# An encoder layer's recurrence: block-diagonal state in the chain, and small matmuls on different tiles of the array issued alternately

## The chip, the cores and the metric

The kernel runs on one core of a Trainium2 chip. Its time is device microseconds (us) of one launch. TensorE is named PE in the profile, VectorE DVE, ScalarE ACT, GpSimd POOL, and SyncE's DMA queue SP.

## What is computed

One layer of a hybrid encoder over 512 frames and 16 meta tokens, 1024 wide: a token mixer (sparse attention beside an RWKV-7 recurrence of 8 heads of 64), then a mixture of 16 experts. The change touches the recurrence alone. Per head, with a state S of 64 x 64:

```python
def step(S, inp):
    r_t, w_t, kk_t, a_t, v_t, k_t = inp
    sa = jnp.einsum('bhvk,bhk->bhv', S, -kk_t)
    S = S * w_t[:, :, None, :] + sa[..., None] * (kk_t * a_t)[:, :, None, :] + v_t[..., None] * k_t[:, :, None, :]
    y = jnp.einsum('bhvk,bhk->bhv', S, r_t)
    return S, y
```

w, kk, a, v, k and r come from projections of the input; y is normalized per head, gated, and merged with the attention's output.

## The kernel before

**Stages.** The recurrence is done in 9 chunks of 64 tokens (the meta tokens with padding are chunk 0), in two halves of four heads. A half is two pairs of heads (`pair_ops`), then `solve`, then `chain`. The list `PLAN` (L749) names the steps: pairs 0 and 1, the attention's index scores, solve of half 0, chain of half 0, gates, pairs 2 and 3, top-k, solve of half 1, the projections for the attention, chain of half 1 with the first two blocks of the attention. After that come the other attention blocks, the branch merge (L931), the output projection with routing (L1138 on), and the experts (L1227 to L1380).

**Order.** The steps are written in this order, but a scheduler sorts each engine's instructions when the program is built, from its own estimate of durations. In the recurrence it fills gaps on PE with projections in three pieces (L268) and with attention scores (L714 and L715). [...]

**Layout.** A pair of heads lies on partitions 0 to 63 and 64 to 127. A matmul whose operands lie on 64 partitions uses half of the array's rows, one whose result has 64 partitions half of its columns. The profile writes a matmul's use of the array as rows*columns ("64*64"), and shows each of these f32 matmuls as two rows: `px` has 144 rows in the trace and 72 instructions in the program.

**pair_ops.** `pwa` (L380) multiplies the low-rank inputs: the decay's on partitions 0 to 63, the other's on 64 to 127, each in two token pieces, one after the other. `pgr` (L431) makes the 128 x 128 products inside a chunk, up to four chunks of one head, then those of the other; DVE masks them into `gram` (L432).

**solve.** DVE inverts 32 x 32 triangles in 31 steps (L475, L477); the result goes through DRAM into `gram`. Then PE works with small blocks: `pmg` and `pmh` (L493, L499, 36 of 32 x 32 each), then per two chunks `px` (L508, heads on rows and columns 64 to 127), copied by ACT to `x0`, and `pu` (L524, rows and columns 0 to 63), copied to `avt`. `pwt` (L518) is 32 products once per half, head by head; the head of a pair picks the result's 64 columns of the array.

**chain.** This is the sequential part. For each chunk after the first: DVE decays the state S into `ds` (L536); PE makes `pcu` from `rav` and `ds`, two matmuls for the heads on partitions 0 to 63, two for the others (L542), each two added to `avt` by DVE (L543); PE makes the new state's products `pcs` (L547, neighbouring heads on different columns of the array); DVE adds them to `ds` (L551). The output `pcy` is made for every chunk and head from two matmuls, L563 (128 rows of the array) and L565 (64 rows), which accumulate. Two PSUM banks hold it over two chunks; then DVE takes statistics and normalizes (L577 to L582). These banks, and those of `pcu`, `pcs` and the attention scores, come from one group of three (`ps`).

Of the kernel before, what the change touches and what calls it, by code (L numbers as in the profile page):

```python
# [21 lines left out]
NTOK = T + NM  # L22
# [47 lines left out]
def trunk(ctx, tc, I, out, probe=None):  # L70
# [292 lines left out]
    def pair_ops(H, p, us):  # L363
# [12 lines left out]
        for dst, ro, cb, pad in ((sg, 0, p, -1.0), (ta, 64, 4 + p, 0.0)):  # L376
            G.memset(dst[:, 0, NM:64], pad)
            for t0, t1 in ((0, HA), (HA, NTOK)):
                b = bank("pwa", PB)
                PE.matmul(b[:, 0:t1 - t0], waup[ro:ro + 64, cp], xs[ro:ro + 64, t0:t1], start=True, stop=True)  # L380
                if t0 == 0:
# [62 lines left out]
    def solve(H):  # L444
# [44 lines left out]
        for q0 in range(0, Q, 16):  # L489
            m = min(16, Q - q0)  # L490
            b = bank("pmg").rearrange("p (q s) -> p q s", q=16)
            for q in range(m):
                PE.matmul(b[32:64, q, :], gq[0:32, q0 + q, 96:128], pm1[0:32, q0 + q, :], start=True, stop=True)  # L493
            A.activation(pm1[32:64, q0:q0 + m], b[32:64, 0:m], AF.Copy)
        for q0 in range(0, Q, 16):
            m = min(16, Q - q0)
            b = bank("pmh").rearrange("p (q s) -> p q s", q=16)
            for q in range(m):
                PE.matmul(b[0:32, q, :], pm1[32:64, q0 + q, :], gq[32:64, q0 + q, 96:128], start=True, stop=True)  # L499
            A.activation(gq[0:32, q0:q0 + m, 96:128], b[0:32, 0:m], AF.Copy)  # L500


        for c0 in range(0, NCH, 2):
            m = min(2, NCH - c0)
            b = bank("px").rearrange("p (c h f) -> p c h f", c=2, h=4)
            for c in range(m):
                for h in range(4):
                    PE.matmul(b[64:128, c, h, :], gram[64:128, h, c0 + c, 64:128], avt[64:128, c0 + c, h * 64:h * 64 + 64],  # L508
                              start=True, stop=True)
            x0 = rt.tile([64, 2, 4, 64], F32, name="x0", tag="lp")  # L510
            A.activation(x0[:, 0:m], b[64:128, 0:m], AF.Copy)
            if c0 == 0:
                for a in range(2):
                    bw = bank("pwt").rearrange("p (c t) -> p c t", c=8)
                    for h in range(2):
                        hh = 2 * a + h
                        for c in range(8):
# [3 lines left out]
            b = bank("pu").rearrange("p (c h f) -> p c h f", c=2, h=4)  # L521
            for c in range(m):
                for h in range(4):
                    PE.matmul(b[0:64, c, h, :], gram[0:64, h, c0 + c, 64:128], x0[:, c, h, :], start=True, stop=True)  # L524
            A.activation(avt[0:64, c0:c0 + m, :], b[0:64, 0:m].rearrange("p c h f -> p c (h f)"), AF.Copy)

    def chain(H):
        hf = H.hf
        gram, bkt, avt, rav = H.gram, H.bkt, H.avt, H.rav
        S = None  # L530
        yb = None
        late = None
        for c in range(NCH):
            if c:
                ds = rk.tile([128, 2, 64], F32, name="ds", bufs=2)
                V.tensor_tensor(ds, S, H.dc[:, :, c].unsqueeze(2).to_broadcast([128, 2, 64]), op=ALU.mult)  # L536
                av = avt[0:64, c, :].rearrange("p (a b f) -> p a b f", a=2, b=2)
                for h in range(2):
                    hs = slice(h * 64, h * 64 + 64)
                    b = bank("pcu", CB[0]).rearrange("p (a f) -> p a f", a=8)[0:64, 0:2, :]  # L540
                    for a in range(2):
                        PE.matmul(b[:, a, :], rav[hs, a, c, 64:128], ds[hs, a, :], start=True, stop=True)  # L542
                    V.tensor_tensor(av[:, :, h, :], b, av[:, :, h, :], op=ALU.add)  # L543
            if c < NCH - 1:
# [5 lines left out]
                if c:  # L550
                    V.tensor_tensor(S, b, ds, op=ALU.add)  # L551
                else:
                    V.tensor_copy(S, b)
# [4 lines left out]
            if cr % 2 == 0:  # L558
                yb = [bank("pcy", CB[2]).rearrange("p (a f) -> p a f", a=8)[:, 0:2, :] for _ in range(2)]
            ts = slice((cr % 2) * 64, (cr % 2) * 64 + 64)  # L560
            for h in range(4):
                hs = slice((h % 2) * 64, (h % 2) * 64 + 64)
                PE.matmul(yb[h % 2][ts, h // 2, :], gram[:, h, c, 0:64], avt[:, c, h * 64:h * 64 + 64],  # L563
                          start=True, stop=False)
                PE.matmul(yb[h % 2][ts, h // 2, :], rav[hs, h // 2, c, 0:64], ds[hs, h // 2, :],  # L565
                          start=False, stop=True)
            if cr % 2 == 0:
                if late:
                    late()
                    late = None  # L570
                yield
                continue
            i = cr // 2
            st = rk.tile([128, 4, 6], F32, name="gst", bufs=2)
            mv = rk.tile([128, 12], F32, name="gmv", bufs=2)
            for h in range(4):
                V.bn_stats(st[:, h, :], yb[h % 2][:, h // 2, :])  # L577
# [3 lines left out]
            for h in range(4):  # L581
                V.tensor_scalar(ytm[:, h * 64:h * 64 + 64], yb[h % 2][:, h // 2, :],  # L582
# [973 lines left out]
```

## Time and profile before

| | us |
|---|---|
| median of 3 runs | 1021.57 |
| lowest, highest | 1017.36, 1031.18 |
| time of the profiled execution | 1017.48 |
| its span, first to last instruction | 1015.7 |

The profile is one execution. "Busy" is the time in which an engine has an instruction of the program in work. Matmuls overlap, so how fast they follow one another is read from starts in the timeline, and a group's busy time counts an overlapped stretch once. [...]

### The profile page before, as it was taken

The numbers are of one execution on the slowest core, as the hardware profiler recorded it, in microseconds if no ns is written. First come the engines' busy times: TensorE is split into PE (matmuls) and PEld (weight loads), VectorE is DVE, ScalarE is ACT, GpSimd is POOL, SyncE is SP. The second block draws the span as 40 slices with busy tenths as digits, with TensorE's granted clock in tenths as the row PEclk, the third lists the DMA queues.
The fourth block names the chain that finished last, engine by engine and source line by source line (L and its number), as shares of the span: only waits on it lengthen the run. The fifth ranks groups of instructions, "written<-read, shape, count | busy, mean of one in ns | idle before, by whom it ended". The sixth has DMA issues, their size and how long they took to land. (4 is left out here: it accounts for less than half of the span.)

```text
span 1015.7 us, 14994 instructions
## 1 busy us (share of the span) xinstructions
PE 932.4 (92%) x5441; PEld 730.8 (72%) x5441; DVE 714.2 (70%) x1525; ACT 492.0 (48%) x801; POOL 286.0 (28%) x251
## 2 busy tenths in 40 slices
PE   4888999999989989999999999957999999999994
PEld 3877866886777777866556878746887878877772
DVE  8767299956677694134473453877999899899876
ACT  4524275332214123513262332225888888888861
POOL 5444144312244142102132610461121221211203
PEclk9999799958989798967999999878999999999997
DMA  6311113502010124201004879429899999999822
GB/s 238 104 49 42 43 42 96 163 32 63 22 42 25 39 80 85 64 1 34 30 32 155 293 251 356 158 89 369 306 327 346 356 336 356 348 337 346 304 75 105
DMA packets 46111, 166.05 MB, mean 163 GB/s; under 512 B 15523, under 2 KB 15651, under 8 KB 33744
## 3 DMA queue, kind: packets, MB, share of 16 engines
q1 hardware_dynamic: 40016, 151.90, 41.8%
q0 software_dynamic: 6016, 13.13, 4.5%
q8 instruction: 45, 0.74, 0.3%
q14 instruction: 34, 0.28, 0.1%
HBM read 151.25 MB, written 21.62 MB: 170 GB/s over the span
## 5 line engine op out<-in xcount | busy, mean ns | idle before, releaser
L251 POOL TENSOR_TENSOR wlo<-wraw,whi 128x512 fp32r<-128x512 f32 x92 | 130.0, 1421 | 235.4 <-ACT whi L250 188.6
L1228 DVE TENSOR_TENSOR wlo<-ering,whi 128x1024 fp32r<-128x1024 f32 x123 | 149.1, 1221 | 25.7 <-ACT whi L1227 12.7
L1227 ACT ACTIVATE whi<-ering 128x1024 fp32r<-128x1024 f32 x123 | 130.3, 1060 | 40.1 <-PE ph L1242 30.8
L268 PE MATMUL pa<-hthi,whi 128*128 128x512 f32 (+1 forms) x304 | 120.9, 398 | 5.5 <-DVE q L820 4.2
L268 PE MATMUL pa<-hthi,wlo 128*128 128x512 f32 (+1 forms) x304 | 118.8, 391 | 0.0
L268 PE MATMUL pa<-htlo,whi 128*128 128x512 f32 (+1 forms) x304 | 118.7, 391 | 0.0
L250 ACT ACTIVATE whi<-wraw 128x512 fp32r<-128x512 f32 x92 | 57.1, 628 | 92.0 <-PE pa L268 39.0
L1180 POOL DMA_INDIRECT acc_dram<-y,gix x15 | 23.8, 1584 | 219.6 <-ACT y L1380 219.6
L268 PEld LDWEIGHTS pa<-hthi,whi 128*128 128x128 f32 x304 | 63.7, 210 | 17.5 <-issue 5.4
L1228 DVE TENSOR_TENSOR wxl<-ering,wxh 128x1024 fp32r<-128x1024 f32 x59 | 72.0, 1220 | 5.6 <-ACT wxh L1227 5.3
L268 PEld LDWEIGHTS pa<-htlo,whi 128*128 128x128 f32 x304 | 63.8, 210 | 9.8 <-issue 1.2
L268 PEld LDWEIGHTS pa<-hthi,wlo 128*128 128x128 f32 x304 | 63.3, 208 | 9.8 <-issue 1.5
L1227 ACT ACTIVATE wxh<-ering 128x1024 fp32r<-128x1024 f32 x59 | 62.5, 1060 | 16.2 <-PE ph L1242 12.4
L1242 PE MATMUL ph<-whi,xl 128*128 128x512 f32 x156 | 62.6, 401 | 7.0 <-DVE xl L1192 7.0
L1242 PE MATMUL ph<-whi,xh 128*128 128x512 f32 x156 | 64.8, 415 | 0.0
L1242 PE MATMUL ph<-wlo,xh 128*128 128x512 f32 x156 | 62.4, 400 | 0.0
L1370 PE MATMUL py<-whi,hhl 128*128 128x512 f32 x188 | 58.8, 394 | 0.0
L1370 PEld LDWEIGHTS py<-whi,hhl 128*128 128x128 f32 x188 | 35.1, 188 | 8.2
L1242 PEld LDWEIGHTS ph<-whi,xl 128*128 128x128 f32 x156 | 29.8, 191 | 13.3 <-DVE xl L1192 7.5
L1242 PE MATMUL ph<-wxh,xl 128*128 128x512 f32 x92 | 36.6, 397 | 0.9 <-DVE xl L1192 0.9
L268 PE MATMUL pb<-hthi,whi 128*128 128x256 f32 x128 | 37.2, 291 | 0.0
L268 PE MATMUL pb<-htlo,whi 128*128 128x256 f32 x128 | 37.2, 290 | 0.0
(456 smaller groups left out, 2240.7 us busy)
## 6 DMA issues: line engine op xcount, KB each, us to landing
ering<-in_we_dram SPq DMA_DIRECT2D x91, 1024.0 KB
wraw<-in_w_t_dram SPq DMA_DIRECT2D x49, 512.0 KB
eringx<-in_we_dram SPq DMA_DIRECT2D x5, 1024.0 KB
gt<-g_dram SPq DMA_DIRECT2D x16, 256.0 KB
xt<-in_x_dram SPq DMA_DIRECT2D x4, 512.0 KB
h_dram<-xt SPq DMA_DIRECT2D x4, 512.0 KB
ering<-in_w_t_dram SPq DMA_DIRECT2D x2, 1024.0 KB
hx<-h_dram SPq DMA_DIRECT2D x4, 512.0 KB
```

The source lines that it names most:

```text
L250: A.activation(hi, src, AF.Copy)
L251: eng.tensor_tensor(lo, src, hi, op=ALU.subtract)
L268: PE.matmul(dst, w[k // 4][:, k % 4, 0:m], x[:, k, t0:t1], start=(k == 0 and j == 0), stop=(k == KT - 1 and j == 2))
L1180: pin(G.indirect_dma_start(out=acc_dram[:, :], out_offset=bass.IndirectOffsetOnAxis(ap=gix[:, e:e + 1], axis=0), in_=ys.pop(e), in_offset= ...
L1227: pin(A.activation(hi, src, AF.Copy))
L1228: pin(V.tensor_tensor(lo, src, hi, op=ALU.subtract))
L1242: pin(PE.matmul(hb, x[:, k, :], ww, start=(k == 0 and j == 0), stop=(k == KT - 1 and j == 2)))
L1370: pin(PE.matmul(yb_[hh], x[:, kk, :], ww, start=(kk == 0 and j == 0), stop=(kk == 3 and j == 2)))
```

## The change

- In `chain`, `ds` becomes `dsb`: per pair a 128 x 128 block with one head's state in the upper left and the other's in the lower right, zeros elsewhere (cleared once by POOL, four buffers in turn). DVE writes it in two instructions of 64 partitions, and adds the new state in two as well.
- `pcu` is now two matmuls of 128 rows and 128 result columns, added to `avt` in one DVE instruction.
- `pcy` is issued once for two chunks, into one PSUM bank: first the eight products with `gram`, then four with `dsb`, alternating between the two chunks, which lie on different columns of the array.
- `pwa`, `pgr` and `pwt` alternate between the two heads or inputs; `pmh` alternates with the `pmg` of the next 16 blocks, and `pu` with the `px` of the next two chunks, with two `x0` buffers in one tile.

```diff
-            for t0, t1 in ((0, HA), (HA, NTOK)):
-                b = bank("pwa", PB)
+        for t0, t1 in ((0, HA), (HA, NTOK)):
+            bs = [bank("pwa", PB) for _ in low]
+            for b, (dst, ro, cb, pad) in zip(bs, low):
                 PE.matmul(b[:, 0:t1 - t0], waup[ro:ro + 64, cp], xs[ro:ro + 64, t0:t1], start=True, stop=True)
...
-            for h in range(2):
-                hs = slice(h * 64, h * 64 + 64)
-                b = bank("pgr", PB).rearrange("p (c t) -> p c t", c=4)
-                for c in range(m):
-                    PE.matmul(b[:, c, :], bk[hs, c0 + c, :], rv[hs, c0 + c, 0:128], start=True, stop=True)
+            bs = [bank("pgr", PB).rearrange("p (c t) -> p c t", c=4) for _ in range(2)]
+            for c in range(m):
+                for h in range(2):
+                    hs = slice(h * 64, h * 64 + 64)
+                    PE.matmul(bs[h][:, c, :], bk[hs, c0 + c, :], rv[hs, c0 + c, 0:128], start=True, stop=True)
...
+        steps = [(c0, min(2, NCH - c0)) for c0 in range(0, NCH, 2)]
+        for n in range(len(steps) + 1):
+            todo = []
+            if n < len(steps):
+                c0, m0 = steps[n]
+                bx = bank("px").rearrange("p (c h f) -> p c h f", c=2, h=4)
+                todo += [(c * 4 + h, bx[64:128, c, h, :], gram[64:128, h, c0 + c, 64:128],
+                          avt[64:128, c0 + c, h * 64:h * 64 + 64]) for c in range(m0) for h in range(4)]
+            if n:
+                c1_, m1 = steps[n - 1]
+                x0 = x0s[:, (n - 1) % 2]
+                bu = bank("pu").rearrange("p (c h f) -> p c h f", c=2, h=4)
+                todo += [(c * 4 + h + 0.5, bu[0:64, c, h, :], gram[0:64, h, c1_ + c, 64:128], x0[:, c, h, :])
+                         for c in range(m1) for h in range(4)]
+            for _, b, l, r in sorted(todo, key=lambda x: x[0]):
+                PE.matmul(b, l, r, start=True, stop=True)
...
-                ds = rk.tile([128, 2, 64], F32, name="ds", bufs=2)
-                V.tensor_tensor(ds, S, H.dc[:, :, c].unsqueeze(2).to_broadcast([128, 2, 64]), op=ALU.mult)
-                av = avt[0:64, c, :].rearrange("p (a b f) -> p a b f", a=2, b=2)
+                ds = dsb[0][:, c % 4]
                 for h in range(2):
                     hs = slice(h * 64, h * 64 + 64)
-                    b = bank("pcu", CB[0]).rearrange("p (a f) -> p a f", a=8)[0:64, 0:2, :]
-                    for a in range(2):
-                        PE.matmul(b[:, a, :], rav[hs, a, c, 64:128], ds[hs, a, :], start=True, stop=True)
-                    V.tensor_tensor(av[:, :, h, :], b, av[:, :, h, :], op=ALU.add)
+                    V.tensor_tensor(ds[hs, :, h, :], S[hs], H.dc[hs, :, c].unsqueeze(2).to_broadcast([64, 2, 64]), op=ALU.mult)
+                b = bank("pcu", CB[0])[0:64, 0:256]
+                for a in range(2):
+                    PE.matmul(b[:, a * 128:a * 128 + 128], rav[:, a, c, 64:128], ds[:, a].rearrange("p h f -> p (h f)"),
+                              start=True, stop=True)
+                V.tensor_tensor(avt[0:64, c, :], b, avt[0:64, c, :], op=ALU.add)
...
+            yb = bank("pcy", CB[2]).rearrange("p (h f) -> p h f", h=8)[:, 0:4, :]
+            ts = [(slice(q * 64, q * 64 + 64), c - 1 + q) for q in range(2)]
+            for h in range(4):
+                for t_, cc in ts:
+                    PE.matmul(yb[t_, h, :], gram[:, h, cc, 0:64], avt[:, cc, h * 64:h * 64 + 64], start=(h == 0), stop=False)
+            for a in range(2):
+                for t_, cc in ts:
+                    PE.matmul(yb[t_, 2 * a:2 * a + 2, :], rav[:, a, cc, 0:64], dsb[0][:, cc % 4, a], start=False, stop=(a == 1))
```

What the scheduler makes of it on PE in the chain of half 1, about chunks 1 and 2 (`psq` are attention scores, `pcu`, `pcs` and `pcy` the chain's products, named above). Before:

```order
L563 MATMUL pcy<-avt,gram 64x64
L565 MATMUL pcy<-ds,rav_2128 64x64
L714 MATMUL psq<-k_3978,q_3803 128x144
L542 MATMUL pcu<-ds,rav_2128 64x64 x2
L715 MATMUL psq<-kl,q_3803 128x144
L714 MATMUL psq<-k_3978,q_3803 128x144
L542 MATMUL pcu<-ds,rav_2128 64x64 x2
L563 MATMUL pcy<-avt,gram 64x64
L565 MATMUL pcy<-ds,rav_2128 64x64
```

Now:

```order
L562 MATMUL pcu<-dsb,rav_2081 64x128 x2
L736 MATMUL psq<-k_3903,q_3741 128x144
L737 MATMUL psq<-kl,q_3741 128x144
L736 MATMUL psq<-k_3903,q_3741 128x144
L568 MATMUL pcs<-avt,bkt 64x64 x4
L591 MATMUL pcy<-avt,gram 64x64 x8
L594 MATMUL pcy<-dsb,rav_2081 64x128 x4
L737 MATMUL psq<-kl,q_3741 128x144
```

The pairs of `pcy`, four to a chunk, have become one run of eight and one of four for two chunks, and the two parts of `pcu` are one.

On PE in the solve of half 1 (`pwt`, `px` and `pu` as above, `pa` the projections that fill). Before:

```order
L518 MATMUL pwt<-gram,avt 64x64 x32
L524 MATMUL pu<-x_3372,gram 64x64 x8
L508 MATMUL px<-avt,gram 64x64 x8
L268 MATMUL pa<-hthi,wlo 128x512
L268 MATMUL pa<-hthi,whi 128x512
L268 MATMUL pa<-htlo,whi 128x512
L268 MATMUL pa<-hthi,wlo 128x512
L268 MATMUL pa<-hthi,whi 128x512
L524 MATMUL pu<-x_3429,gram 64x64 x8
```

Now:

```order
L528 MATMUL px<-avt,gram 64x64
L528 MATMUL pu<-x_3316,gram 64x64
L528 MATMUL px<-avt,gram 64x64 x8
L268 MATMUL pa<-htlo,whi 128x512
L268 MATMUL pa<-hthi,wlo 128x512
L528 MATMUL pu<-x_3316,gram 64x64 x8
L528 MATMUL px<-avt,gram 64x64
L528 MATMUL pu<-x_3316,gram 64x64
```

Single `px` and `pu` alternate (the first two and the last two rows are the ends of runs of eight each), while the `px` of a later step, which waits for nothing, has been moved up in a run of its own, and the run of `pu` stands behind the projections.

On DVE in the chain of half 0 (`MAX` and `MATCH_REPLACE` are the attention's top-k). Before:

```order
L536 TENSOR_TENSOR ds<-S,dc 128x128
L665 MATCH_REPLACE acc_1589<-m_3651,acc_1589 128x400
L665 MATCH_REPLACE acc_1595<-m_3768,acc_1595 128x528
L543 TENSOR_TENSOR avt<-pcu,avt 64x2x64 x2
L664 MAX m_3651<-acc_1589 128x8
L551 TENSOR_TENSOR S<-pcs,ds 128x128
```

Now:

```order
L559 TENSOR_TENSOR dsb<-S,dc 64x2x64 x2
L686 MAX m_3600<-acc_1585 128x8
L687 MATCH_REPLACE acc_1591<-m_3706,acc_1591 128x528
L564 TENSOR_TENSOR avt<-pcu,avt 64x256
L687 MATCH_REPLACE acc_1585<-m_3600,acc_1585 128x400
L686 MAX m_3706<-acc_1591 128x8
L574 TENSOR_TENSOR S<-pcs,dsb 64x128 x2
```

Decay and state update are two instructions each, the addition to `avt` is one, and two instructions of the top-k stand between it and the state update.

## Rows read from the trace of the kernel before

**Rows 1.** The page: busy time of each engine with its share of the span, and the granted clock in 40 slices of 25.4 us, in tenths.

```profile
PE 932.4 (92%) x5441; PEld 730.8 (72%) x5441; DVE 714.2 (70%) x1525; ACT 492.0 (48%) x801; POOL 286.0 (28%) x251
...
PEclk9999799958989798967999999878999999999997
```

**Rows 2.** Busy time by stretch: from:to and length in us, busy us (instructions) of PE, its weight loads, DVE, ACT and POOL, granted clock, DMA share, GB/s. The stretches are: pairs 0 and 1; solve of half 0 on PE; its chain; pairs 2 and 3; solve of half 1 on DVE; the same on PE; its chain; rest of the attention and the merge; output projection and routing; experts.

```profile
40.00:120.00 80.00, 72.37 (x572) 63.44 (x573) 48.70 (x80) 30.77 (x70) 27.88 (x28) 0.93 0.16 52
...
187.00:231.00 44.00, 43.96 (x418) 36.64 (x416) 29.54 (x105) 13.59 (x25) 8.00 (x10) 0.67 0.25 77
231.00:297.00 66.00, 64.45 (x454) 49.15 (x452) 45.04 (x144) 16.14 (x36) 21.04 (x21) 0.91 0.13 41
297.00:349.00 52.00, 46.15 (x403) 38.69 (x402) 35.53 (x67) 16.63 (x37) 16.71 (x14) 0.90 0.13 42
349.00:397.00 48.00, 42.40 (x214) 35.57 (x214) 41.14 (x78) 12.89 (x24) 16.13 (x12) 0.90 0.30 75
397.00:428.00 31.00, 30.76 (x404) 26.04 (x406) 0.00 (x0) 12.79 (x23) 5.11 (x4) 0.94 0.25 71
428.00:501.00 73.00, 72.33 (x398) 48.30 (x398) 31.64 (x170) 20.93 (x56) 12.97 (x11) 0.79 0.08 22
501.00:599.00 98.00, 96.34 (x413) 64.32 (x411) 51.40 (x167) 43.00 (x104) 36.08 (x26) 0.98 0.45 159
599.00:693.00 94.00, 73.82 (x368) 61.10 (x369) 58.20 (x196) 23.75 (x31) 30.64 (x31) 0.86 0.58 221
693.00:1016.00 323.00, 303.00 (x1397) 240.51 (x1395) 282.44 (x290) 246.28 (x291) 60.80 (x37) 0.98 0.83 300
```

**Rows 3.** Groups of PE instructions from 40 to 600 us: line, tile written and read, use of the array, operands, count | busy us, mean ns of one | idle before.

```profile
L431 PE MATMUL pgr<-rav,bk 64*128 64x128 f32 x144 | 20.7, 345 | 2.2 <-POOL rav L420 2.2
L524 PE MATMUL pu<-x,gram 64*64 64x64 f32 x144 | 14.2, 268 | 0.0
L542 PE MATMUL pcu<-ds,rav 64*64 64x64 f32 x128 | 13.8, 245 | 1.5 <-DVE avt L543 1.5
L508 PE MATMUL px<-avt,gram 64*64 64x64 f32 x144 | 13.4, 258 | 0.0
L547 PE MATMUL pcs<-avt,bkt 128*64 128x64 f32 x128 | 10.1, 260 | 0.0
L518 PE MATMUL pwt<-gram,avt 64*64 64x64 f32 x128 | 9.4, 268 | 0.0
L462 PE MATMUL plp<-ident,gram 32*36 32x32 f32 x256 | 8.8, 226 | 0.0
L493 PE MATMUL pmg<-pm,gram 32*32 32x32 f32 x144 | 4.9, 191 | 0.9 <-DMA pm<-msc 0.9
```

**Rows 4.** Sums over stretches for one tile alone: first `pcy` (187 to 297 and 428 to 501 us), then `pwa` (40 to 345 us); PE, its weight loads, and the engine that reads the tile.

```profile
sum 183.00, PE 37.97 PEld 26.96 DVE 14.99; mean PE 18.98 PEld 13.48 DVE 7.49
...
sum 305.00, PE 8.16 PEld 4.55 ACT 7.82; mean PE 8.16 PEld 4.55 ACT 7.82
```

**Rows 5.** PE in order of time in the chain of half 0 (start, us from first start to last end, line, tiles, use of the array, count).

```profile
243.55 0.45 PE L547 MATMUL pcs<-avt,bkt 128*64 128x64 f32 x8
243.84 0.28 PE L563 MATMUL pcy<-avt,gram 128*64 128x64 f32 x2
244.05 0.33 PE L565 MATMUL pcy<-ds,rav 64*64 64x64 f32 x2
244.30 0.33 PE L563 MATMUL pcy<-avt,gram 128*64 128x64 f32 x2
```

**Rows 6.** The same view in the solve: first in half 0, then in half 1.

```profile
209.89 1.59 PE L508 MATMUL px<-avt,gram 64*64 64x64 f32 x13
...
212.43 0.63 PE L268 MATMUL pa<-hthi,wlo 128*128 128x512 f32 x1
...
416.11 0.22 PE L508 MATMUL px<-avt,gram 64*64 64x64 f32 x1
416.11 0.22 PE L524 MATMUL pu<-x,gram 64*64 64x64 f32 x1
416.16 0.22 PE L508 MATMUL px<-avt,gram 64*64 64x64 f32 x1
...
416.22 0.92 PE L508 MATMUL px<-avt,gram 64*64 64x64 f32 x13
417.07 0.50 PE L268 MATMUL pa<-hthi,wlo 128*128 128x512 f32 x1
...
417.64 0.39 PE L268 MATMUL pa<-htlo,whi 128*128 128x512 f32 x1
```

**Rows 7.** The same view in the attention: transposes on all columns or on 16, with 128 result columns, and the instruction behind them.

```profile
495.58 1.04 PE L731 MATMUL ppt<-ident,S 128*16 128x128 f32 x8
496.37 0.48 PE L268 MATMUL pa<-htlo,whi 128*128 128x512 f32 x1
```

**Rows 8.** The same view in pair 0: four chunks of `pgr` for both heads.

```profile
64.08 1.71 PE L431 MATMUL pgr<-rav,bk 64*128 64x128 f32 x16 [0.84 <-POOL rav L420]
```

**Rows 9.** Waits from 187 to 501 us: engine, line, what it waited for, us in total, times, longest.

```profile
PE pcu L542 <- DVE avt L543: 1.5, 1, 1.5
...
DVE avt L543 <- PE pcu L542: 18.7, 22, 1.9
```

**Rows 10.** Groups of DVE instructions from 187 to 501 us, columns as in rows 3.

```profile
L543 DVE TENSOR_TENSOR avt<-pcu,avt 64x128 f32<-64x128 f32 x32 | 8.7, 280 | 18.8 <-PE pcu L542 18.7
L536 DVE TENSOR_TENSOR ds<-S,dc 128x128 f32<-128x128 f32 x16 | 4.4, 273 | 0.0
```

More of the change, by code (lines that the diff above doesn't have):

```diff
@@ L375, in pair_ops @@
         sg, ta = T3("sg"), T3("ta")
[L376 removed]
+        low = ((sg, 0, p, -1.0), (ta, 64, 4 + p, 0.0))
+        for dst, ro, cb, pad in low:
             G.memset(dst[:, 0, NM:64], pad)
[L378 to L379 removed]
+        for t0, t1 in ((0, HA), (HA, NTOK)):
+            bs = [bank("pwa", PB) for _ in low]
+            for b, (dst, ro, cb, pad) in zip(bs, low):
                 PE.matmul(b[:, 0:t1 - t0], waup[ro:ro + 64, cp], xs[ro:ro + 64, t0:t1], start=True, stop=True)
+            for b, (dst, ro, cb, pad) in zip(bs, low):
                 if t0 == 0:
@@ L488, in solve @@
                          fsc[b * 64:b * 64 + Q].rearrange("q s t -> s q t"))
[L489 to L500, printed above, removed]
@@ L503, in solve @@
[L503 to L512, printed above, removed]
+        steps = [(q0, min(16, Q - q0)) for q0 in range(0, Q, 16)]
@@ new lines, in solve @@
+        for n in range(len(steps) + 1):
+            todo = []
+            if n < len(steps):
+                q0, m0 = steps[n]
+                bg = bank("pmg").rearrange("p (q s) -> p q s", q=16)
+                todo += [(q, bg[32:64, q, :], gq[0:32, q0 + q, 96:128], pm1[0:32, q0 + q, :]) for q in range(m0)]
+            if n:
+                q1, m1 = steps[n - 1]
+                bh = bank("pmh").rearrange("p (q s) -> p q s", q=16)
+                todo += [(q + 0.5, bh[0:32, q, :], pm1[32:64, q1 + q, :], gq[32:64, q1 + q, 96:128]) for q in range(m1)]
+            for _, b, l, r in sorted(todo, key=lambda x: x[0]):
+                PE.matmul(b, l, r, start=True, stop=True)
+            if n < len(steps):
+                A.activation(pm1[32:64, q0:q0 + m0], bg[32:64, 0:m0], AF.Copy)
+            if n:
+                A.activation(gq[0:32, q1:q1 + m1, 96:128], bh[0:32, 0:m1], AF.Copy)
@@ new lines, in solve @@
+        x0s = rt.tile([64, 2, 2, 4, 64], F32, name="x0", tag="lp")
+        steps = [(c0, min(2, NCH - c0)) for c0 in range(0, NCH, 2)]
+        for n in range(len(steps) + 1):
+            todo = []
+            if n < len(steps):
+                c0, m0 = steps[n]
+                bx = bank("px").rearrange("p (c h f) -> p c h f", c=2, h=4)
+                todo += [(c * 4 + h, bx[64:128, c, h, :], gram[64:128, h, c0 + c, 64:128],
+                          avt[64:128, c0 + c, h * 64:h * 64 + 64]) for c in range(m0) for h in range(4)]
+            if n:
+                c1_, m1 = steps[n - 1]
[3 more added lines that the diff above has]
+                         for c in range(m1) for h in range(4)]
+            for _, b, l, r in sorted(todo, key=lambda x: x[0]):
+                PE.matmul(b, l, r, start=True, stop=True)
+            if n < len(steps):
+                A.activation(x0s[:, n % 2, 0:m0], bx[64:128, 0:m0], AF.Copy)
+            if n == 0:
@@ L513, in solve @@
                 for a in range(2):
                     bw = bank("pwt").rearrange("p (c t) -> p c t", c=8)
-                    for h in range(2):
-                        hh = 2 * a + h
-                        for c in range(8):
+                    for c in range(8):
+                        for h in range(2):
+                            hh = 2 * a + h
                             PE.matmul(bw[h * 64:h * 64 + 64, c, :], avt[0:64, 1 + c, hh * 64:hh * 64 + 64],
@@ L520, in solve @@
                     A.activation(rav[:, a, 1:NCH, 64:128], bw, AF.Copy)
[L521 to L525, printed above, removed]
+            if n:
+                A.activation(avt[0:64, c1_:c1_ + m1, :], bu[0:64, 0:m1].rearrange("p c h f -> p c (h f)"), AF.Copy)
+    dsb = []
     def chain(H):
@@ L529, in chain @@
         gram, bkt, avt, rav = H.gram, H.bkt, H.avt, H.rav
+        if not dsb:
+            dsb.append(rk.tile([128, 4, 2, 2, 64], F32, name="dsb", bufs=1))
+            G.memset(dsb[0], 0.0)
         S = None
-        yb = None
         late = None
@@ L550, in chain @@
                 if c:
-                    V.tensor_tensor(S, b, ds, op=ALU.add)
+                    for h in range(2):
+                        hs = slice(h * 64, h * 64 + 64)
+                        V.tensor_tensor(S[hs], b[hs], ds[hs, :, h, :], op=ALU.add)
                 else:
@@ L558, in chain @@
             if cr % 2 == 0:
[L559 to L567, printed above, removed]
                 if late:
```

5 lines of the change are left out of this document (3 added, 2 removed).

## The prediction

> **What bounds the kernel now.** I read the page first, then busy time by stretch, then the groups of PE instructions, then PE in order of time where the change works. The page shows PE busy 92% of the span [rows 1]. The stretches show where that is a bound: in the solves, the chains and the merge PE is busy 97% or more of the time (43.96 of 44 us, 64.45 of 66, 30.76 of 31, 72.33 of 73, 96.34 of 98), and DVE at most 68% of it [rows 2]. Between 297 and 397, where pairs 2 and 3 and the inversion on DVE stand, PE has gaps: it is busy 88.6 of 100 us, DVE 76.7 [rows 2]. In the chain the waits say the same from the other side: DVE waited for `pcu` 18.7 us in 22 pieces, PE for DVE's addition once, 1.5 us [rows 9]. So the chain, though sequential, is not held by its hand-overs: PE always has projections or attention scores between its steps, and what PE spends there moves everything behind it. Behind the chain of half 1 come attention and merge, again PE; the experts' weights are requested after that, so they move along.
>
> **The clock.** It is at the low level for part of the recurrence: the mean is 0.67 in the first solve, 0.94 in the second, which has the same instructions, 0.91 and 0.79 in the chains [rows 2]. A projection row lasts 0.63 us at the low level and 0.39 at the full one [rows 6].
>
> **The change, part by part** (savings are PE time between 40 and 501 us).
>
> *`pcy`.* It holds PE 37.97 us, in 256 rows, that is 4.75 per two chunks [rows 4]. Each run of two rows takes 0.21 to 0.26 us from its start to the next one's, and each changes the use of the array, L563 to 128*64, L565 to 64*64 [rows 5]. `pcs` beside it is what the new order looks like: 128 rows, 64 columns, neighbours on different columns: eight rows in 0.29 us to the next start, 36 ns each [rows 5]. Now there are 16 such rows for two chunks (0.58 us), and 8 rows with 128 columns. For those the transposes give the upper price, 0.79/8 = 99 ns [rows 7], and half of that, because neighbours alternate, the lower; I take 65 ns (0.52 us), nearer the lower, since alternation takes `px`, (417.07-416.22)/13 = 65 ns a row in a run of its own kind, to 25 to 30, two rows in 0.05 us [rows 6]. With 0.2 us for entering and leaving, 1.3 us for two chunks, 10.4 in all at full clock and some 12 at the mixed one: saved **26** (bounds 22 and 29).
>
> *`pcu`.* 13.8 us in 128 rows, 0.86 per chunk [rows 3]. Now four rows of 128 columns on the same columns of the array: 4 x 0.099 + 0.2 = 0.6. Saved 16 x 0.26 = **4** (0 to 7).
>
> *`px`, `pu`.* 27.6 us in 288 rows [rows 3]; a run of its own kind costs 65 ns a row at full clock and 1.59/13, about 120, at the low one, alternation 25 to 30 [rows 6]. But the order shows that about 64 of 144 rows per half alternate; the rest stand in runs as before. 128 x 35 = 4.5, part of which overlaps already: **4** (1 to 8).
>
> *`pwt`.* 9.4 us in 128 rows [rows 3]; priced like `pcs`, 36 to 60 ns by clock, it takes 6: **3** (0 to 5).
>
> *`pgr`, `pwa`.* Two heads on different rows of the array. `pgr` is 20.7 us [rows 3]; 16 rows take 1.71 us, 107 ns each [rows 8]. If the heads overlapped fully, half of it would go; no row tells how much of that the present order has already at the change of head, so I take a quarter: **5** (0 to 10). `pwa` likewise: 8.16 [rows 4], **2** (0 to 4). Both now hold two banks at once, which DVE and ACT empty one after the other as before.
>
> *`pmg`, `pmh`.* Nothing: 4.9 us / 144 = 34 ns in runs, and `plp`, which alternates already, 8.8 / 256 = 34 [rows 3]. Their new order waits for ACT once more, behind projections; if that cover went, two copies of 0.6 us.
>
> Sum of PE time: 26+4+4+3+5+2 = **44** (23 to 63).
>
> *What comes off.* `pgr` and `pwa` stand in stretches where PE has gaps: half of their 7 is taken as not reaching the end, 4. On DVE each chunk has a second decay and a second state update, and one addition less. The decay takes 0.27 us for all 128 partitions [rows 10], and one of half the partitions takes no less by the 64-partition addition, 0.28 [rows 10]; between `pcs` and the next `pcu` that is two instructions more, about 0.4 us at the pace of a queue. It was hidden behind PE; with PE shorter by 2 to 3 us per chunk, PE may now wait for it, behind the top-k or softmax instructions that the order puts ahead. All of it exposed is 16 x 0.4 = 6 us, and I take 6; bounds 0, and 15 if one other DVE instruction of 0.6 us is exposed as well. Behind `pcu` stand, on PE, the projections and scores that would be held up. POOL's one clearing of `dsb` waits for nothing and lies ahead of the first chain, where POOL is busy 8 of 44 us [rows 2]: nothing. `pcy` holds one PSUM bank for a short time instead of two over two chunks; I count that as nothing, though it can only make `pcs` and `psq` freer.
>
> Net: 44 - 4 - 6 = **34**. Against the profiled execution's 1017.5 us that is 983.5. The median of the runs is 4 us above that execution, so I say **985**.
>
> [...]The new `pcy` and `pwt` differ only in columns of the array, not in rows. `pcs` does the same and costs 36 ns a row, `px` in a run of its own tile 65 [rows 5, 6]. [...]
>
> **The rivals.**
>
> *Columns alone do not overlap for these operands.* Then `pcy` costs 16 x 0.065 + 8 x 0.099 + 0.2 = 2.0 us per two chunks, 16 in all, four to six more than above, and `pwt` gains nothing: 985 + 8 = 993. [...] 6%.
>
> *The clock gains too.* At the low level lie (1-0.67) x 2 x 44 = 29 us of the first solve, 12 and 31 of the chains [rows 2]. If the shorter stretches of small matmuls leave half of these 72 us at full clock, each of them did only 0.39/0.63 of the work: 36 x 0.38 = 14. 970. For it speaks that the second solve stays high with the same work, so that it is near the edge. 18%.
>
> *DVE becomes the bound of half 0.* Between 231 and 397 us DVE is busy 121.7 of 166 [rows 2], with top-k and inversion in long sequences. If the solve of half 1 starts no earlier than now, only what is saved after 397 counts: half of `pcy`, `pcu`, `px`, `pu` and `pwt`, 18, less 3: 1002. Against it: DVE has gaps of 44 us there. 16%.
>
> *Slower: the clock falls.* Between the small matmuls of the solve now stand fewer projections, 2 or 3 where 5 stood. If the second solve falls to the low level as the first does, it costs 44 - 31 = 13 us [rows 2]. If the chains, which then have some 66 us at full clock left, fall too, 66 x (0.63/0.39 - 1) = 40. Together 53 against 34: 1037. It decides from about 34/0.62 = 55 us more at the low level, a mean clock below some 0.75 between 187 and 501 us, where it is 0.85 now. 8%.
>
> That the change does not do what it says is excluded for the chain by the order, and counted for `px` and `pu`.
>
> **How the numbers follow.** The forecast, 985 with a range of its own of 968 to 1001 from the bounds of the terms, has 52%. About 2% is what a measurement of this kernel can tell from no change: 1001 and 1042. Faster: 0.47 of the forecast, 0.18 of the clock's gain, 0.05 of the rule's, 0.06 of the DVE case: 0.76. Slower: most of the clock's fall, 0.05. Within: 0.19. The range 962 to 1008 leaves out the clock's fall, the best end of its gain, and the worst of the DVE case.
>
> **What would show it.** `pcy` on PE should fall from 37.97 us to 10 to 14, its 64-column rows following each other at about 36 ns; `pcu` to 9 or 10; `pwt` to 6. The chain of half 1 should take some 55 us instead of 73. DVE's waits for `pcu` should shrink, and PE's for DVE grow to no more than 6 us over both chains. The merge, the routing and the experts should keep their lengths, 98, 94 and 323 us. The prediction is wrong in its cause if the chains shorten by 20 us and the start of the experts does not move, or if the mean clock from the first solve to the end of the second chain moves by over 0.05.

## The result, and the profile after

The changed kernel was timed in three comparisons, each beside the kernel before. In the first, right after the prediction, its median was 980.43 us (971.65 to 990.88, 4 runs) against 1026.38: ratio 0.9552, 95% interval 0.9414 to 0.969. Two repetitions gave 983.6 against 1018.5 (0.9719, 0.9644 to 0.9794) and 982.59 against 1018.37 (0.9676, 0.962 to 0.9731). Over all three: 982.4 us (14 runs) against 1019.7 (25 runs), **37 us less**. The prediction said 985, and 34 less than the profiled execution. The ratios and their intervals use only executions within 1.5% of the fastest of their kernel, so they are not ratios of these medians.

The profile read here is of the third comparison: 984.8 us by its own time, so 32.7 us less than the execution of [rows 1 to 10]. Its page:

```profile
span 983.1 us, 14758 instructions
...
PE 884.5 (90%) x5313; PEld 692.3 (70%) x5313; DVE 730.0 (74%) x1539; ACT 491.8 (50%) x801; POOL 290.4 (30%) x252
```

Against [rows 1], PE is busy 47.9 us less (932.4 to 884.5), and its gaps are 15.3 us longer (1015.7 - 932.4 = 83.3, now 98.6). The difference is the gain: 32.6 us of span.

Where it came from, by stages cut at the same work in both kernels. Columns as in [rows 2]; the stages are: up to the first `pmg`; PE's part of the first solve; its chain; pairs 2 and 3 with the second inversion; PE's part of the second solve; its chain; attention and merge; output projection and routing; experts. First the kernel before:

```profile
0.00:189.00 189.00, 161.25 (x998) 131.74 (x998) 141.25 (x321) 86.59 (x180) 79.38 (x88) 0.95 0.29 92
189.00:230.00 41.00, 40.96 (x398) 34.44 (x398) 27.54 (x95) 12.67 (x23) 7.00 (x9) 0.65 0.24 77
230.00:288.00 58.00, 56.45 (x422) 42.29 (x420) 39.42 (x124) 14.29 (x31) 17.86 (x17) 0.94 0.15 47
288.00:397.00 109.00, 97.54 (x656) 82.00 (x655) 82.29 (x164) 31.66 (x65) 36.20 (x29) 0.88 0.20 53
397.00:428.00 31.00, 30.76 (x404) 26.04 (x406) 0.00 (x0) 12.79 (x23) 5.11 (x4) 0.94 0.25 71
428.00:489.00 61.00, 60.84 (x343) 41.55 (x343) 26.93 (x154) 17.71 (x49) 8.17 (x7) 0.75 0.09 27
489.00:595.00 106.00, 104.99 (x455) 69.05 (x455) 53.20 (x173) 44.06 (x105) 40.87 (x30) 0.98 0.40 139
595.00:682.00 87.00, 72.66 (x372) 60.22 (x371) 55.99 (x196) 24.34 (x34) 28.84 (x30) 0.89 0.55 212
682.00:1016.00 334.00, 307.00 (x1407) 243.41 (x1405) 287.57 (x299) 247.87 (x292) 62.60 (x39) 0.97 0.83 299
```

and the changed one:

```profile
0.00:189.00 189.00, 157.71 (x998) 127.86 (x998) 142.04 (x320) 86.51 (x180) 84.19 (x89) 0.95 0.28 92
189.00:219.00 30.00, 29.90 (x381) 25.45 (x380) 24.75 (x89) 11.54 (x21) 5.96 (x8) 0.70 0.34 108
219.00:273.00 54.00, 48.23 (x381) 37.76 (x382) 45.18 (x134) 15.84 (x34) 19.38 (x17) 0.91 0.17 50
273.00:379.00 106.00, 91.68 (x654) 76.74 (x650) 85.97 (x170) 31.44 (x64) 35.38 (x30) 0.90 0.19 54
379.00:404.00 25.00, 25.00 (x377) 21.57 (x376) 0.00 (x0) 11.08 (x20) 3.86 (x3) 0.86 0.18 57
404.00:453.00 49.00, 46.83 (x316) 31.05 (x315) 33.72 (x160) 19.57 (x53) 10.39 (x9) 0.90 0.16 49
453.00:560.00 107.00, 103.92 (x448) 66.92 (x445) 54.77 (x174) 43.68 (x103) 39.75 (x30) 0.98 0.39 138
560.00:647.00 87.00, 72.62 (x372) 60.05 (x371) 56.03 (x197) 24.35 (x34) 28.33 (x29) 0.89 0.56 212
647.00:983.00 336.00, 308.65 (x1409) 244.86 (x1408) 287.57 (x299) 247.81 (x292) 63.12 (x40) 0.97 0.83 298
```

The lengths change by 0, -11, -4, -3, -6, -12, +1, 0 and +2 us. Read the second column of numbers beside the first: up to 189 us PE is busy 3.5 us less, and the length is the same. In the first chain PE is busy 8.2 us less and the stretch is 4 shorter; DVE is now busy 45 of its 54 us. With pairs 2 and 3 it is 5.9 and 3. In the two solves and the second chain, where PE had no gaps, nearly all of it became time. A length alone misleads: the first solve has 11 us less also because fewer projections stand in it, which are done later, and the second chain has 12 us less also because its granted clock is 0.90, not 0.75.

The groups on PE, 40 to 600 us, columns as in [rows 3]:

```profile
L434 PE MATMUL pgr<-rav,bk 64*128 64x128 f32 x144 | 15.0, 351 | 5.1 <-POOL rav L423 4.4 <-DVE gram L436 0.7
L562 PE MATMUL pcu<-dsb,rav 128*64 128x128 f32 x64 | 11.1, 300 | 4.5 <-DVE dsb L559 4.4
L568 PE MATMUL pcs<-avt,bkt 128*64 128x64 f32 x128 | 7.5, 240 | 0.0
L537 PE MATMUL pwt<-gram,avt 64*64 64x64 f32 x128 | 7.4, 313 | 0.0
L610 PE MATMUL pyt<-ident,ytm 128*128 128x128 f32 x16 | 5.1, 319 | 5.3 <-DVE ytm L604 5.3
```

Sums over 40 to 600 us of what overlaps itself or has several groups, in turn line 528 (`px` and `pu` together), `pcy` and `pwa`:

```profile
40.00:600.00 560.00, 21.33 (x288) 0.92 0.28 94
...
40.00:600.00 560.00, 10.59 (x192) 0.92 0.28 94
...
40.00:600.00 560.00, 7.45 (x32) 0.92 0.28 94
```

`pcy` in order of time, as [rows 5]:

```profile
230.87 0.45 PE L568 MATMUL pcs<-avt,bkt 128*64 128x64 f32 x8
231.16 0.64 PE L591 MATMUL pcy<-avt,gram 128*64 128x64 f32 x16
231.62 0.61 PE L594 MATMUL pcy<-dsb,rav 128*64 128x128 f32 x8
232.16 0.50 PE L268 MATMUL pa<-htlo,whi 128*128 128x512 f32 x1
```

All of `pcy` for two chunks takes 1.00 us (231.16 to 232.16): 16 rows in 0.46, 29 ns each, and 8 rows with 128 columns in 0.54, 68 ns each with the change to the projection behind them. Inside the run of sixteen the trace's starts come in pairs, 6 to 7 ns apart and 51 to 52 ns to the next pair: one row on either column half.

### The profile page after: what moved, and what is told of

It reads as the page before. It is cut to its first block, busy times and chain, and to the rows that moved or that the text cites. A ratio compares the mean times of both kernels' runs of the same rounds, so it can differ in the third digit from the quotient of the medians.

```text
span 989.1 us, 14758 instructions
## 1 busy us (share of the span) xinstructions
PE 891.0 (90%) x5313; PEld 694.9 (70%) x5313; DVE 731.4 (74%) x1539; ACT 492.0 (50%) x801; POOL 290.6 (29%) x252
## 5 line engine op out<-in xcount | busy, mean ns | idle before, releaser
L251 POOL TENSOR_TENSOR wlo<-wraw,whi 128x512 fp32r<-128x512 f32 x92 | 132.3, 1447 | 215.2 <-ACT whi L250 213.1
L1249 ACT ACTIVATE whi<-ering 128x1024 fp32r<-128x1024 f32 x123 | 130.2, 1059 | 42.2 <-PE ph L1264 33.2
L268 PE MATMUL pa<-hthi,whi 128*128 128x512 f32 (+1 forms) x304 | 118.2, 389 | 5.4 <-DVE q L842 4.1
L1197 POOL DMA_INDIRECT xg<-x_dram,gix x15 | 30.2, 2012 | 26.3 <-PE pet L1345 19.6
```

What stands on the lines that cost most here:

```text
L251: eng.tensor_tensor(lo, src, hi, op=ALU.subtract)
L268: PE.matmul(dst, w[k // 4][:, k % 4, 0:m], x[:, k, t0:t1], start=(k == 0 and j == 0), stop=(k == KT - 1 and j == 2))
L1197: pin(G.indirect_dma_start(out=xg, out_offset=None, in_=x1_dram[:, :], in_offset=bass.IndirectOffsetOnAxis(ap=gix[:, e:e + 1], axis=0), bo ...
L1249: pin(A.activation(hi, src, AF.Copy))
```

## The experiments

Where expectations count PE time "from start to next start", every row lasts until the next one on PE begins (or until its own end, before a gap). So no stretch is counted twice, as it is where busy times of groups that overlap are added. By this measure `pcy` is 34.9 us in the kernel before and 9.8 in the changed one (in the profile of the first comparison), `pcu` 11.8 and 9.8, `pgr` 19.8 and 14.0, and all small matmuls of the recurrence 130 and 91.

### 1. The chain alone, and the alternations alone

The first kernel has the `chain` of the changed one and the rest of the kernel before, the second the reverse.

> The chain's part of the change alone (block-diagonal dsb, merged pcu, pcy of two chunks); solve, pgr and pwa as before. Theory (the gain is the chain's rows on PE): pcy falls from 34.9 us of PE time, from start to next start, to 9 to 12, pcu from 11.8 to about 10; 25 to 30 us less than the kernel before, ratio 0.97 to 0.976. Rival (the whole gain of 4.5% needs the alternation in the solve, or the clock): under 15 us, ratio over 0.985.

> The alternations alone (pwa, pgr, pmg and pmh, px and pu, pwt); the chain as before. Theory: pgr 20 to 14 us, pwt 8.7 to 6.5, px and pu together 22 to 20, so 10 us of PE time, of which some 8 reach the end: ratio 0.99 to 0.995. Rival (the small matmuls of the solve carry much of the gain, through the clock): ratio under 0.982.

The chain alone: 995.96 us against 1027.89 (17 runs), ratio 0.9725 (0.9614 to 0.9836); `pcy` 9.4, `pcu` 10.5 us. The alternations alone: 1008.1 us, 0.9868 (0.9774 to 0.9963); `pgr` 13.5, `pwt` 6.5, `px` and `pu` 22.2, `pcy` 35.8 as before. Both are as the theories had them within their intervals, but that of the alternations, 0.977 to 0.996, reaches to its rival (under 0.982) too. The product of the two ratios, 0.960, lies inside the interval of the whole change in the first comparison and just below the other two. By these ratios the chain carries about two thirds.

### 2. Grouping `pcy` by its use of the array

```diff
             for h in range(4):
-                hs = slice((h % 2) * 64, (h % 2) * 64 + 64)
-                PE.matmul(yb[h % 2][ts, h // 2, :], gram[...], avt[...], start=True, stop=False)
+                PE.matmul(yb[h % 2][ts, h // 2, :], gram[...], avt[...], start=(h < 2), stop=False)
+            for h in range(4):
+                hs = slice((h % 2) * 64, (h % 2) * 64 + 64)
                 PE.matmul(yb[h % 2][ts, h // 2, :], rav[...], ds[...], ...)
```

> The kernel before with one edit: within a chunk the gram rows of pcy (128*64) are issued first and the rav rows (64*64) behind them, so that the use of the array changes twice or four times a chunk and not eight times. Same instructions, same data. Theory (the change of the array's use between neighbours is what pcy paid for, 0.15 to 0.2 us for each pair of changes): 34.9 us of PE time fall to 17 to 23, ratio 0.983 to 0.99. Rival (what counts is that neighbours write the same columns, so that nothing overlaps, or the number of rows): pcy stays over 30, ratio over 0.995.

Measured: `pcy` 21.4 us, as the theory had it. The time is 1009.58 us against 1027.89 by the medians, 0.982, at the edge of what was expected; the ratio 0.9725 (0.9646 to 0.9804), which is more than expected, rests on 4 of the 14 executions, so the size of the gain in time stays open. One chunk, PE in order of time (the first of its 16 rows starts 0.06 us earlier):

```profile
260.41 0.57 PE L562 MATMUL pcy<-avt,gram 128*64 128x64 f32 x7
260.91 0.45 PE L566 MATMUL pcy<-ds,rav 64*64 64x64 f32 x8
261.29 0.39 PE L268 MATMUL pa<-htlo,whi 128*128 128x272 f32 x1
```

These 15 rows take 59 ns each, against 105 to 130 where the use of the array changes after every two [rows 5]. Inside the first run the starts are 58 to 59 ns apart (all on the same columns), at the change from L562 to L566 152 ns, and in the second run they come in pairs again, 6 to 7 ns apart and, behind the first pair, 52 to the next: the two heads lie on different rows of the array. In the kernel before, at the place of [rows 5], each change costs 148 to 152 ns, and the row behind it follows after 106 to 107. It costs the same from L565 to L563, which writes another bank, as from L563 to L565, which adds to what L563 has just written; so it is not the accumulation that is paid for. So 13 to 14 us of `pcy`'s fall, over half of it, needs neither the block-diagonal state nor two chunks together, only fewer changes of the use. What PE does in the 152 ns no run shows.

### 3. The compact state, two chunks together

The kernel before, with `ds` in four buffers and `pcy` issued once for two chunks:

```diff
+            for h in range(4):
+                for t_, cc in ts:
+                    PE.matmul(yb[h % 2][t_, h // 2, :], gram[:, h, cc, 0:64], avt[...], start=(h < 2), stop=False)
+            for h in range(4):
+                hs = slice((h % 2) * 64, (h % 2) * 64 + 64)
+                for t_, cc in ts:
+                    PE.matmul(yb[h % 2][t_, h // 2, :], rav[hs, h // 2, cc, 0:64], dss[cc][hs, h // 2, :], ...)
```

> The kernel before with pcy of two chunks issued together, 8 gram rows alternating between column halves, then 8 rav rows going round the four quadrants; the state stays compact (no block-diagonal dsb, no added DVE instruction), pcu as before. Theory (grouping and alternation are the gain, the block-diagonal form is not needed for pcy): pcy 9 to 13 us of PE time, ratio 0.972 to 0.98. Rival (without the block-diagonal state the 64-row rows stay dear): pcy over 18 us, ratio over 0.985.

Measured: 993.46 us, 0.9739 (0.9658 to 0.982), `pcy` 9.1 us, as the theory said:

```profile
259.67 0.64 PE L569 MATMUL pcy<-avt,gram 128*64 128x64 f32 x16
260.24 0.46 PE L574 MATMUL pcy<-ds,rav 64*64 64x64 f32 x16
260.63 0.62 PE L408 MATMUL pss<-sq,hsel 128*32 128x256 f32 x2
```

Sixteen rows of a quarter of the array take 0.39 us, 24 ns each, with the change behind them. Inside the run the starts come in fours, one row on each quadrant within 20 ns, and the last fours follow each other after 58 to 59 ns: 15 ns a row. The ratio is level with the chain of the change (0.9725), so the block-diagonal state is not what brings the time.

### 4. Columns not alternating

```diff
-            for h in range(4):
-                for t_, cc in ts:
+            for t_, cc in ts:
+                for h in range(4):
                     PE.matmul(yb[t_, h, :], gram[...], avt[...], start=(h == 0), stop=False)
```

and the same for the rows with `dsb`.

> The changed kernel, with pcy issued chunk by chunk: the same 16 rows, four gram rows on one column half, then four on the other, and so with the rav rows. Theory (neighbours on different columns overlap): gram rows 36 ns become 60 to 65, rav rows 80 become 95 to 105; pcy from 9.8 to 14 or 15 us of PE time; the time 3 to 5 us more, which one look can't tell. [...]

`pcy` 12.8 us: the L591 rows 58 ns on average (36 in the changed kernel), the L594 rows 85 (80). Two chunks, PE in order of time:

```profile
254.71 0.74 PE L591 MATMUL pcy<-avt,gram 128*64 128x64 f32 x13
255.23 0.32 PE L594 MATMUL pcy<-dsb,rav 128*64 128x128 f32 x1
255.28 0.28 PE L591 MATMUL pcy<-avt,gram 128*64 128x64 f32 x2
255.39 0.27 PE L594 MATMUL pcy<-dsb,rav 128*64 128x128 f32 x1
255.40 0.22 PE L591 MATMUL pcy<-avt,gram 128*64 128x64 f32 x1
255.46 0.60 PE L594 MATMUL pcy<-dsb,rav 128*64 128x128 f32 x6
255.99 0.39 PE L268 MATMUL pa<-hthi,whi 128*128 128x272 f32 x1
```

The 24 rows take 1.28 us, not 1.00. So the alternation of columns is worth 3 us, a little less than expected, because PE undoes part of the order of its list (where the products stand four and four, then two and two): from the fifth row on, rows of the second column half start 4 to 6 ns behind rows of the first, and L594 rows of the first half start ahead of the last L591 rows of the second. So rows on different columns ran side by side in this run, and PE did not start them in the order of its list (the first L594 row at 255.23 us, the L591 rows behind it at 255.28). The one time taken, 993.08 us, decides nothing.

### 5. Fewer DVE instructions in a chunk

```diff
-                for h in range(2):
-                    hs = slice(h * 64, h * 64 + 64)
-                    V.tensor_tensor(ds[hs, :, h, :], S[hs], H.dc[hs, :, c]..., op=ALU.mult)
+                V.tensor_tensor(ds, S, dcm[:, :, :, c].unsqueeze(3).to_broadcast([128, 2, 2, 64]), op=ALU.mult)
...
-                for h in range(4):
-                    PE.matmul(b[(h % 2) * 64:(h % 2) * 64 + 64, h // 2, :], bkt[:, c, h * 64:h * 64 + 64], ...)
+                for a in range(2):
+                    PE.matmul(b[:, a].rearrange("p h f -> p (h f)"), bkt[:, c, a * 128:a * 128 + 128], ...)
...
-                        V.tensor_tensor(S[hs], b[hs], ds[hs, :, h, :], op=ALU.add)
+                    V.tensor_tensor(S, b, ds, op=ALU.add)
```

> The changed kernel once more, beside the next two. Theory: median 975 to 990 us, and over its executions the time falls as the mean granted clock rises (990.9 us at 0.925, 971.7 at 0.952 so far); its trace shows the same PE time in the small matmuls, about 91 us, whatever the clock behind the second chain does.

> The changed kernel with fewer DVE instructions in a chunk, three where it has five: pcs issues two rows of 128 columns per chunk and fills the whole block-diagonal shape (its cross terms included), S keeps that shape, and the decay multiplies by a table that is zero off the diagonal, so that dsb is one instruction and the update of S one. Theory (the two DVE instructions that the change added are exposed, the first chain has 7 us of gaps on PE with DVE busy 48 of 55 us): PE's idle time from 200 to 300 us falls from 10 to 4 or 5, the two chains together take 4 to 8 us less than 97.5, 3 to 8 us less in all, ratio to the kernel before 0.945 to 0.951. Rival (PE's gaps are filled by moved projections anyway, or pcs costs more in 128-column rows): no gain, ratio 0.955 or over.

The changed kernel beside it: 983.6 us, its small matmuls 86.9 us of PE time, less than the 91 that the expectation held to be fixed: they follow the clock too. From 188 to 452 us 0.90 of it is granted there, where the profile of the first comparison, with the 91, has 0.88; and in the kernel before a `px` row in a run of its own starts every 58 to 59 ns at 1.00 (416.2 to 416.9 us) and every 106 to 107 at 0.50 (209.9 to 211.2). With three DVE instructions: **975.34 us**, 0.958 (0.9492 to 0.9668), a gain, but not as expected. Stages 3 and 6 of its profile (the two chains):

```profile
215.00:266.00 51.00, 46.52 (x369) 37.73 (x368) 43.47 (x128) 16.25 (x35) 20.85 (x20) 1.00 0.16 52
...
396.00:445.00 49.00, 48.02 (x276) 33.52 (x274) 29.62 (x145) 19.21 (x53) 10.65 (x9) 0.86 0.16 49
```

PE's gaps in the chains are 4.5 and 1.0 us, where the changed kernel has 5.8 and 2.2; from 200 to 300 us they did not fall at all (11.0, 10.2 in the run beside it). The two chains together are 100 us long, as in the profile of the changed kernel beside it (the 97.5 of the expectation was too low for that one already). So two DVE instructions more per chunk hold PE up by 2 to 3 us, not 6, and where the rest of the 8 us lies is not settled: against the profile shown above no stage differs by more than 3 us, and against the one beside it, 5.1 us slower, PE is busy as long (877.5 and 877.4 us) and of the 5.3 us that its gaps are longer 2.5 lie before the first solve, ahead of the code that was edited. The intervals of the two ratios overlap.

### 6. All alternations with the compact state

Experiment 3's `pcy`, `pcu` of both heads issued alternately into two banks, and all other parts of the change.

> The compact state with pcy in the four quadrants (as in the run before), pcu's two heads issued alternately in two banks, and all other alternations of the change: no block-diagonal state. Theory (the block-diagonal state is not what brings the time): small matmuls 88 to 94 us of PE time like the changed kernel's 91, PE's idle time some 5 us less, ratio 0.948 to 0.956. Rival (one bank for pcu and pcy and one addition per chunk are what the block-diagonal form is good for): ratio 0.965 or over.

975.92 us, 0.9606 (0.953 to 0.9683), 8 us below the changed kernel beside it and level with experiment 5; small matmuls 85.6 us, PE's gaps 96.1 us in all against the 100.1 of the changed kernel beside it. The theory stands, with a ratio a little over its range and small matmuls a little under theirs; the interval of the ratio still reaches to the rival's 0.965.

### 7. The transposes behind the chain's output, a chunk later

Waits of the changed kernel from 189 to 453 us, columns as in [rows 9]: DVE's for `pcu`, which led there, and PE's two inside the chains:

```profile
DVE avt L564 <- PE pcu L562: 6.3, 4, 3.1
...
PE pyt L610 <- DVE ytm L604: 4.9, 5, 1.4
...
PE pcu L562 <- DVE dsb L559: 4.4, 4, 1.9
```

```diff
-YB, YD = "ps", (0, 0)
+YB, YD = "ps", (1, 1)
```

It was made in the changed kernel and in those of 5 and 6.

> The changed kernel a third time, as the measure for the three that follow on the same chip: ratio to the kernel before 0.955 to 0.972.

> The changed kernel with one constant changed: the transposes pyt of a pair of chunks are issued a chunk later, behind the next chunk's pcs. Theory (with PE shorter, PE stands in its order before pyt and waits for the ten DVE instructions behind pcy: 5 us between 214 and 320 us in the changed kernel's trace, 0.6 us in the second chain): the waits of pyt for ytm fall below 1 us, the time by 2 to 5 us. Rival (the wait only moves, to pcu for dsb, as DVE is what the first chain runs by): dsb's wait grows by as much, the time stays within 2 us of the changed kernel beside it.

> Three DVE instructions per chunk (the full block-diagonal S) and the later pyt together. Theory: both waits of PE in the first chain, for ytm and for dsb, go; PE's idle time from 200 to 300 us under 8 us (10 in the changed kernel), 8 to 12 us less time than the changed kernel beside it. Rival: the gaps of the first chain belong to the pair that runs beside it (gram, rav, sq), and nothing is gained over the run without the later pyt, which was 8 us below the changed kernel by the medians, with intervals that overlap.

> The compact state, pcy in four quadrants, pcu alternating in two banks, all other alternations, and the later pyt. Theory (the block-diagonal state is not needed): 5 to 12 us below the changed kernel beside it, the second chain about 40 us where the changed kernel takes 49. Rival: as the run without the later pyt, 8 us below by the medians, or level with the changed kernel.

The changed kernel 982.59 us, with the later transposes 983.08 (0.9719, 0.9648 to 0.979); the kernel of 5 974.18 (0.9576, 0.9506 to 0.9646), that of 6 976.31 (0.9599, 0.953 to 0.9667): each within 1.2 us of itself without the edit. Four stages of the changed kernel with the edit (first chain, pairs 2 and 3, second chain, merge):

```profile
210.00:251.00 41.00, 37.46 (x332) 28.55 (x330) 36.23 (x117) 13.26 (x30) 11.69 (x10) 1.00 0.17 52
251.00:366.00 115.00, 98.68 (x699) 82.59 (x695) 92.64 (x187) 33.97 (x69) 44.92 (x37) 0.91 0.19 55
...
390.00:431.00 41.00, 39.92 (x297) 27.52 (x296) 31.82 (x154) 18.38 (x50) 9.41 (x8) 0.92 0.12 40
431.00:546.00 115.00, 110.24 (x456) 70.44 (x456) 56.97 (x181) 44.29 (x107) 40.89 (x30) 0.97 0.39 134
```

The chains are 13 and 8 us shorter, and what follows each is 9 and 8 us longer: the scheduler only put projections and attention behind the chain instead of inside it. The wait for `ytm` fell from 4.9 to 3.6 us, not below 1, and the one for `dsb` from 4.4 to 2.2, so neither the theory's size nor the rival's shift is what happened; the time stayed, as the rival had it. In the kernels of 5 and 6 too the later transposes gained nothing over the same kernel without them, as their rivals had it: in that of 5 PE's idle time from 200 to 300 us is 8.6 us (under 8 expected), in that of 6 the second chain takes 44 us (about 40). The kernel of 5 lies 8 us below the changed one in both comparisons, without and with this edit, with intervals that overlap in either; it is the fastest version by the medians, and the compact state of 6 is within 2 us of it.

## Why the prediction was right

The way and the mechanism are as forecast. That the number came so close is in part luck: the small matmuls gave 39.0 us of PE time where 44 had been added up, 15.3 came off where 10 had been taken, and TensorE's clock gave 8.9 on the rest of PE's work, for which the sum had nothing. 39.0 + 8.9 - 15.3 = 32.6, against 34. (983.5 and the 4 us of the median also make 987.5, not the 985 that was said.)

The terms, by the busy time of [rows 3, 4] and of the profile above:

| | before | after | saved | predicted |
|---|---|---|---|---|
| `pcy` | 37.97 | 10.59 | 27.4 | 26 |
| `pcu` | 13.8 | 11.1 | 2.7 | 4 |
| `px`, `pu` | 23.6 | 21.3 | 2.2 | 4 |
| `pwt` | 9.4 | 7.4 | 2.0 | 3 |
| `pgr` | 20.7 | 15.0 | 5.7 | 5 |
| `pwa` | 8.16 | 7.45 | 0.7 | 2 |
| sum | | | 40.7 | 44 |

- **`pcy`.** Both prices held: 29 ns where 36 was taken from `pcs`, and 68, with the leaving, where 65 without it was chosen between 50 and 99. That neighbours on other columns overlap was the step on which it rested; experiments 3 and 4 show it (one row on each of four quadrants within 20 ns, rows of the two column halves 4 to 6 ns apart). That the change of use is dear was read from [rows 5] rightly; experiment 2 measures it (152 ns from start to start, not 58). The 0.2 us for entering and leaving was an estimate; in the profile of the first comparison the projection behind `pcy` starts 0.20 us after its last row (230.55 and 230.76 us), and its first row 0.05 after the last one of `pcs` (229.70 and 229.75).
- **`pcu`.** The step is mis-sized by a little: 0.69 us a chunk, not 0.6.
- **`px`, `pu`.** Half of the 4 us came. The prediction's 27.6 us adds the busy times of two groups that overlap already; in the trace they hold PE 23.6 us together, and the alternation takes off 2.2. With the alternations alone (experiment 1) it is less still, 22.2 us from start to next start against 22.4 in the kernel before; these rows follow the clock too (17.2 in the run beside experiment 5, with 0.76 and 0.93 of the clock granted in its two solves, against 0.70 and 0.86 in the stages above).
- **Not in the sum.** `pcs` fell from 10.1 to 7.5 us of busy time [rows 3] with no edit of its own. From start to next start, which counts nothing twice, the six terms saved 25.0, 2.0, 2.0, 2.2, 5.6 and 0.8 us, `pcs` 1.1, and all small matmuls together 39.0 (130.2 to 91.2). PE's whole saving is 47.9 us; the other 8.9 are the clock's, as said below.
- **What comes off** was 10 in the prediction and is 15.3. Half of `pgr` and `pwa` was to be lost: it is all of it in pairs 0 and 1 (3.5 us) and half in pairs 2 and 3 (2.9 of 5.9). For DVE 6 us were taken; the chains' gaps grew by 4.2 and 2.0. The size is right and its cause only in part: experiment 5 shows 2 to 3 us for two instructions, and the longest wait, `pyt` for `ytm`, was not named. The merge adds 2.1 of gaps.
- **The rivals.** That columns alone do not overlap is ruled out by experiment 4 (starts 4 to 6 ns apart on the two halves). That DVE becomes the bound of half 0, so that nothing gained there counts, did not happen: its solve, its chain and pairs 2 and 3 gave 11 + 4 + 3 us, as much as the second solve and chain with 6 + 12. A trace of it is there, in the first chain and the pairs, where PE's saving of 14 us became 7. The clock's fall did not come, and its gain came in part: from the first solve to the end of the second chain the granted clock is 0.84 before and 0.88 after. In the trace of the kernel before it is 0.50 or 1.00 of the full one at any moment (0.50 from 202 to 235 us, 1.00 from 236 to 286), so these means are (1-0.84) x 2 x 300 = 96 us at the low level and (1-0.88) x 2 x 264 = 63. PE's other rows, 3793 in either kernel, which the change does not touch, take 8.9 us less, 793.3 instead of 802.2. Of this time 93.7 us lay at the low level before and 70.1 after; with 0.39/0.63 of the work done there [rows 6], 23.6 x 0.38 makes 9.0, so the clock accounts for all of it. In the other two profiled executions of the changed kernel, 990.88 and 979.21 us long, these rows save 2.3 and 11.7 us and the small matmuls 39.1 and 43.3. Over the executions the time follows the mean clock, 990.88 us at 0.925 to 971.65 at 0.952 for the changed kernel, 1040.8 at 0.899 to 1007.7 at 0.933 for the one before. What lets the clock rise is not shown.
- **The signs named.** `pcy` 10.6 (10 to 14), `pcu` 11.1 (9 to 10) and `pwt` 7.4 (6), the second chain 12 us shorter by the stages above (73 to 55, so 18, was named), DVE's wait for `pcu` 6.3 (18.7 before), merge, routing and experts 107, 87 and 336 against 106, 87 and 334. PE's waits for DVE in the chains were to be 6 at most, and are 9.3 (4.4 for `dsb`, 4.9 for `ytm`).

## What to carry to other kernels

Before a small matmul is made bigger, look at what its neighbours in PE's list do with the array: sorting them by their use (rows*columns) and letting neighbours lie on different tiles gave as much here as the block-diagonal form (975.92 us in experiment 6, 983.6 for the changed kernel beside it), with no work added elsewhere. Price a saving stage by stage, and take off what lies where PE already has gaps: here PE was busy 48 us less, 9 of them by the clock, and 33 became time. Where groups overlap, add their time from start to next start, not their busy times. A stage's length says little where a scheduler fills it with other work; only the end counts.

## What was not expected of the hardware

- In these runs each tile started a row of 64 result columns every 58 to 59 ns, with one tile in use or more: 58 to 59 ns a row with one (the first run of experiment 2; `px` in the kernel before at 416 us, with 1.00 of the clock granted), 29 with two column halves in turn (`pcy` of the changed kernel), 15 with four quadrants inside their run (experiment 3).
- PE started rows of different column halves out of the order of its list: in experiment 4 the second half's begin behind the fifth of eight rows of the first in six of the eight runs.
- A change between 128*64 and 64*64 cost 152 ns from start to start instead of 58 in experiment 2, and 148 to 152 in the kernel before, where the row behind it followed after 106 to 107. A run of sixteen on the quadrants, with the change behind it, came to 24 ns a row (experiment 3).
